# RWKV chain with both heads of a pair in one full-array TensorE product

## The chip, the cores and the metric

One core of a Trainium2 chip runs the whole program. The metric is device time in microseconds (us) of one execution; lower is better. A core has TensorE (matrix products, results in PSUM banks), VectorE, ScalarE and GpSimd, each with its own instruction queue, and SyncE, which issues the transfers.

## The reference, cut to what matters

One block of a streaming encoder on 512 tokens and 1024 channels: a norm, one input projection, an RWKV-7 branch (8 heads of 64) beside a gated DeltaNet branch (4 heads of 128), a gated merge, an output projection, a gated MLP with a short convolution, a final norm. All is float32. The change concerns the RWKV branch's recurrence:

```python
def step(S, inp):                        # S: (head, value 64, key 64), once per token
    r_t, w_t, k_t, v_t, a_t, b_t = inp
    sa = einsum('bhvk,bhk->bhv', S, a_t)
    S = S * w_t[:, :, None, :] + sa[..., None] * b_t[:, :, None, :] \
        + v_t[..., None] * k_t[:, :, None, :]
    y = einsum('bhvk,bhk->bhv', S, r_t)
    return S, y
...
y = group_norm_heads(y, ln_w, ln_b)      # mean and variance over the 64 channels of a head
y = y + jnp.sum(r_h * k_h * r_k, -1, keepdims=True) * v_h
```

## The kernel before, in words

Activations lie transposed: channels on partitions, 512 tokens along the free axis. The big products (`mm3`, lines 176, 177 and 179, called dense products below) split weights and activations into a high and a low fp32r part and add three products of 128x128 by 512 columns. `unit` fetches the weights and makes the parts `hi` (ScalarE, line 161) and `lo` (GpSimd or VectorE, line 163).

The recurrence is done in 8 chunks of 64 tokens. Two heads share the 128 partitions: head e ("even") on 0 to 63 (`lo`), head o on 64 to 127 (`hi`). A pair of heads is `hp`, 0 to 3; a group `g` is two pairs, and one chain runs over the chunks of both its pairs.
- `rwkv_prep` (steps R0 to R3) builds the operands of a pair: `ase` and `aso` (the decayed a and r of each head), `bkt` (b and k transposed), `ntb`, and the products of all token pairs in a chunk (lines 505 and 506: pair products, four chunks to a group, two groups to a pair of heads), masked by VectorE on line 512. Each of the two products uses 64 of the 128 rows.
- `rwkv_inverse` (steps i0, i1) inverts the triangular 64x64 matrix of every chunk and head and writes it back into `ntb`.
- `rwkv_chain` (steps c0, c1) runs over the chunks. Lines 626 and 627 centre the values (subtract the mean over the channels) and turn tokens to partitions. Per chunk there are three products that depend on one another: the first (639, 640) applies the operands to the state and the values, VectorE copies the result to `Z` (642); the second (645) applies the inverse, VectorE and ScalarE scale the result to U (647, 648); the third (651, 652) makes the next state, which VectorE scales and adds to a copy that ScalarE had scaled (636, 658). State and values lie in one tile for the even head and one for the odd. Lines 605 and 610 make the outputs, for four chunks at a time.

All four products of a step use a part of the array only: 64 columns of outputs (639, 640, 651, 652) or a 64x64 quarter (626, 627, 645):

```python
nc.tensor.matmul(pz[lo, 0, i, :], R[hp]["ase"][:, c, 0, :], se[:, i, 0, :], ...)   # 639
nc.tensor.matmul(pz[hi, 0, i, :], R[hp]["aso"][:, c, 0, :], so[:, i, 0, :], ...)   # 640
```

Before and after the RWKV chain, DeltaNet steps (G, I, C) and projections run. `ORDER` names the steps in program order, and the framework's scheduler writes each engine's queue from it: while the chain waits, TensorE's queue holds dense products of other steps. Waits between engines are put on whole tiles. A pair's operands lie in one buffer `R`, of which there are two (`RB`): the second group's steps and later the merge's gates (line 388) wait for them.

Of the kernel before, what the change touches and what calls it, by code (L numbers as in the profile page):

```python
# [9 lines left out]
F32 = mybir.dt.float32  # L10
# [83 lines left out]
class Body:  # L94
# [328 lines left out]
    def rwkv_prep(self, hp, first=None):  # L423
        nc = self.nc
        Rt, K, r = first or (self.rp.tile([128, 9, T], F32, tag="R", name=self.nm("R")), self.t("P"), self.t("P"))
        ase = Rt[:, 0:2, :].rearrange("p x t -> p (x t)").rearrange("p (c s t) -> p c s t", c=8, s=2)
        aso = Rt[:, 2:4, :].rearrange("p x t -> p (x t)").rearrange("p (c s t) -> p c s t", c=8, s=2)
        ntb = Rt[:, 4:6, :].rearrange("p x t -> p (x t)").rearrange("p (c s t) -> p c s t", c=8, s=2)
        bkt = Rt[:, 6:8, :].rearrange("p x t -> p (x t)").rearrange("p (c t) -> p c t", c=8)
        v = Rt[:, 8, :]  # L430
        if first is None:
            self.shifted(4 + hp, K)
            self.shifted(hp, r)
            self.shifted(8 + hp, v)
# [64 lines left out]
        for h in range(2):  # L499
            pe, po, pt = self.bank(), self.bank(), self.bank()  # L500
            for c in range(4):
                o = slice(c * 128, c * 128 + 128)
                cc = 4 * h + c
                bk = bkh[h][:, c, :, :].rearrange("p s t -> p (s t)")
                nc.tensor.matmul(pe[:, o], bk[0:64], ase[0:64, cc].rearrange("p s t -> p (s t)"), start=True, stop=True)
                nc.tensor.matmul(po[:, o], bk[64:128], aso[64:128, cc].rearrange("p s t -> p (s t)"), start=True, stop=True)
# [4 lines left out]
            for ps, s, tl in ((pe, lo, ntb), (pe, hi, ase), (po, hi, ntb), (po, lo, aso)):  # L511
                nc.vector.tensor_tensor(out=tl[s, w].rearrange("p c s t -> p c (s t)"),  # L512
                                        in0=ps[s, :].rearrange("p (c t) -> p c t", c=4),
                                        in1=rwm[s].unsqueeze(1).broadcast_to([64, 4, 128]), op=ALU.mult)
# [3 lines left out]
        return dict(ase=ase, aso=aso, ntb=ntb, bkt=bkt, v=v)  # L518
# [31 lines left out]
    def rwkv_inverse(self, g, R):  # L550
# [27 lines left out]
        for i, hp in enumerate(hps):  # L578
            ntb = R[hp]["ntb"]
            for q in range(4):  # L580
                s = slice(32 * q, 32 * q + 32)
                o = 32 * (q % 2)
                nc.scalar.activation(ntb[s, :, 0, o:o + 32].rearrange("p g (c j) -> p g c j", j=2), Y[s, 8 * i:8 * i + 8], AF.Copy)
            for b in (0, 64):
                nc.scalar.activation(ntb[b:b + 32, :, 0, 32:64], pfv[b:b + 32, 8 * i:8 * i + 8, :], AF.Copy)

    def rwkv_chain(self, g, R):
# [12 lines left out]
        def outputs(c0, kept):  # L600
            py = self.bank().rearrange("p (i c t) -> p i c t", c=4, i=2)
            for j, (e, o) in enumerate(kept):
                for i, hp in enumerate(hps):
                    for s, tl, a in ((lo, e, "ase"), (hi, o, "aso")):
                        nc.tensor.matmul(py[s, i, j, :], tl[:, i, 0, :], R[hp][a][:, c0 + j, 1, :],
                                         start=(j == 0 and i == 0), stop=False, skip_group_check=True)
            for j, (e, o) in enumerate(kept):
                for i, hp in enumerate(hps):
                    for s, tl in ((lo, e), (hi, o)):
                        nc.tensor.matmul(py[s, i, j, :], tl[s, i, 1, :], R[hp]["ntb"][s, c0 + j, 1, :],  # L610
# [5 lines left out]
        se, so = suv()  # L616
        nc.gpsimd.memset(se[lo, :, 0, :], 0.0)
        nc.gpsimd.memset(so[hi, :, 0, :], 0.0)
        kept = []
        for c in range(8):  # L620
            if c % 4 == 0:
                pv = self.bank().rearrange("p (c i t) -> p c i t", c=4, i=2)
                for c2 in range(4):
                    for i, hp in enumerate(hps):
                        vs = R[hp]["v"][:, (c + c2) * 64:(c + c2) * 64 + 64]
                        nc.tensor.matmul(pv[hi, c2, i, :], vs[lo], cent[lo, 0:64], start=True, stop=True)
                        nc.tensor.matmul(pv[lo, c2, i, :], vs[hi], cent[hi, 64:128], start=True, stop=True)
            c4 = c % 4
            kept.append((se, so))
            for tl, s in ((se, hi), (so, lo)):  # L630
# [438 lines left out]
```

## Time and profile before

| | |
|---|---|
| runs, median (lowest to highest) | 901.0 us (900.7 to 903.66) |
| the profiled execution | 901.19 us, span 899.4 us |
| TensorE busy | 866.2 us (96%) |
| VectorE, ScalarE, GpSimd busy | 590.1, 464.0, 195.4 us |
| mean granted TensorE clock | 0.992 of full |

The span is the time from the first to the last instruction. TensorE's ends are modelled, so the text reads its time from the starts of its products. A product on float32 operands appears as two records with a weight load each; one on fp32r as one. "128*64" in a row is the rows and columns of the array that a product uses.

### The profile page before, as it was taken

The numbers are of one execution on the slowest core, as the hardware profiler recorded it, in microseconds if no ns is written. First come the engines' busy times: TensorE is split into PE (matmuls) and PEld (weight loads), VectorE is DVE, ScalarE is ACT, GpSimd is POOL, SyncE is SP. The second block draws the span as 40 slices with busy tenths as digits, with TensorE's granted clock in tenths as the row PEclk, the third lists the DMA queues.
The fourth block names the chain that finished last, engine by engine and source line by source line (L and its number), as shares of the span: only waits on it lengthen the run. The fifth ranks groups of instructions, "written<-read, shape, count | busy, mean of one in ns | idle before, by whom it ended". The sixth has DMA issues, their size and how long they took to land.

```text
span 899.4 us, 13124 instructions
## 1 busy us (share of the span) xinstructions
PE 866.2 (96%) x4925; PEld 675.9 (75%) x4925; DVE 590.1 (66%) x1156; ACT 464.0 (52%) x879; POOL 195.4 (22%) x182
## 2 busy tenths in 40 slices
PE   7998999999999999999999999999999999999995
PEld 4776777666767777677787888888888888888885
DVE  6799797874888987855486448766666666312125
ACT  7654457667443776583534464444444444323233
POOL 2241123111121221111222213222222222222221
PEclk8999999999999999999999999999999999999998
DMA  6331222121212221135252223332223333223234
GB/s 238 119 105 60 71 71 72 48 72 48 71 59 71 71 72 36 60 113 181 94 188 94 94 76 111 95 94 94 94 94 94 99 103 96 88 88 105 89 106 136
DMA packets 28737, 84.76 MB, mean 94 GB/s; under 512 B 3200, under 2 KB 5376, under 8 KB 28672
## 3 DMA queue, kind: packets, MB, share of 16 engines
q1 hardware_dynamic: 28672, 83.91, 29.3%
q8 instruction: 39, 0.64, 0.3%
q14 instruction: 26, 0.21, 0.1%
HBM read 78.13 MB, written 5.77 MB: 93 GB/s over the span
## 4 chain that ended last, share of the span: by engine, by line
PE 73%; DVE 16%; ACT 4%; issue 3%; DMA 2%; POOL 1%; SPq 0%; DVEq 0%; POOLq 0%; ACTq 0%
PE D L179 20%; PE D L176 20%; PE D L177 20%; DVE R L512 1%; PE A L176 1%; PE A L177 1%; PE A L179 1%; DVE invN L541 1%; DVE lo L163 1%; DVE P L747 1%; DMA raw<-w_in 1%; DVE invY L543 1%; ACT hi L161 1%; DVE R L926 1%; PE B L639 1%
## 5 line engine op out<-in xcount | busy, mean ns | idle before, releaser
L163 POOL TENSOR_TENSOR lo<-raw,hi 128x512 fp32r<-128x512 f32 x133 | 179.8, 1352 | 649.7 <-ACT hi L161 625.8
L161 ACT ACTIVATE hi<-raw 128x512 fp32r<-128x512 f32 (+1 forms) x266 | 165.0, 622 | 257.3 <-PE D L179 193.5
L176 PE MATMUL D<-uh,lo 128*128 128x512 f32 (+1 forms) x456 | 184.0, 405 | 2.7 <-ACT uh L200 1.9
L177 PE MATMUL D<-uh,hi 128*128 128x512 f32 (+1 forms) x456 | 184.1, 405 | 0.0
L163 DVE TENSOR_TENSOR lo<-raw,hi 128x512 fp32r<-128x512 f32 (+1 forms) x133 | 92.4, 695 | 77.2 <-ACT hi L161 76.8
L176 PE MATMUL D<-u2h,lo 128*128 128x512 f32 x352 | 137.9, 392 | 0.0
L177 PE MATMUL D<-u2h,hi 128*128 128x512 f32 x352 | 137.8, 392 | 0.0
L179 PE MATMUL D<-ul,hi 128*128 128x512 f32 (+1 forms) x456 | 135.4, 403 | 0.4 <-DVE ul L198 0.4
L176 PEld LDWEIGHTS D<-uh,lo 128*128 128x128 f32 x456 | 86.2, 189 | 23.5 <-ACT uh L200 2.4
L177 PEld LDWEIGHTS D<-uh,hi 128*128 128x128 f32 x456 | 86.1, 189 | 18.8 <-issue 1.0
L179 PEld LDWEIGHTS D<-ul,hi 128*128 128x128 f32 x456 | 82.6, 188 | 19.6 <-issue 1.2
L179 PE MATMUL D<-u2l,hi 128*128 128x512 f32 x352 | 95.1, 392 | 0.0
L177 PEld LDWEIGHTS D<-u2h,hi 128*128 128x128 f32 x352 | 66.1, 188 | 14.9 <-issue 0.2
L176 PEld LDWEIGHTS D<-u2h,lo 128*128 128x128 f32 x352 | 66.1, 188 | 14.7 <-issue 0.2
L179 PEld LDWEIGHTS D<-u2l,hi 128*128 128x128 f32 x352 | 66.1, 188 | 14.1
L972 DVE SCALAR_TENSOR_TENSOR P<-T,vecs,P 128x511 f32<-128x511 f32 x88 | 69.0, 784 | 8.9 <-ACT P L970 2.8
L969 DVE TENSOR_TENSOR T<-D,acc 128x512 f32<-128x512 f32 x44 | 30.3, 690 | 49.8 <-PE D L179 45.8
L177 PE MATMUL D<-ah,hi 128*128 128x512 f32 (+1 forms) x126 | 45.2, 366 | 0.0
L176 PE MATMUL D<-ah,lo 128*128 128x512 f32 (+1 forms) x126 | 45.1, 366 | 0.0
L541 DVE TENSOR_TENSOR invN<-invA,invY 128x60 f32<-128x60 f32 (+24 forms) x124 | 33.2, 268 | 2.6
L543 DVE TENSOR_TENSOR invY<-invY,invN 128x60 f32<-128x60 f32 (+24 forms) x124 | 32.9, 266 | 2.9
L970 ACT ACTIVATE P<-T,vecs 128x512 f32<-128x512 f32 x44 | 31.8, 723 | 5.4 <-DVE T L969 1.9
(342 smaller groups left out, 1280.1 us busy)
## 6 DMA issues: line engine op xcount, KB each, us to landing
raw<-w_in SPq DMA_DIRECT2D x44, 512.0 KB, 3.6
raw<-ffn_up SPq DMA_DIRECT2D x44, 512.0 KB, 3.5
raw<-ffn_down SPq DMA_DIRECT2D x18, 512.0 KB, 3.5
raw<-w_out SPq DMA_DIRECT2D x8, 512.0 KB, 3.5
spill<-T SPq DMA_DIRECT2D x14, 256.0 KB, 2.0
R<-spill SPq DMA_DIRECT2D x14, 256.0 KB, 5.6
raw<-ffn_down SPq DMA_DIRECT2D x9, 384.0 KB, 3.0
xin<-xT SPq DMA_DIRECT2D x8, 256.0 KB, 5.7
```

Of the source, the lines that this page charges most:

```text
L161: nc.scalar.activation(hi[:, 0:w], raw[:, o:o + w], AF.Copy)
L163: self.on(str(self.halves % 4)).tensor_tensor(out=lo[:, 0:w], in0=raw[:, o:o + w], in1=hi[:, 0:w].bitcast(F32), op=ALU.subtract)
L176: nc.tensor.matmul(ps, wl[:, w[k]], x[k][0], start=(first and i == 0 and k == 0), stop=False)
L177: nc.tensor.matmul(ps, wh[:, w[k]], x[k][0], start=False, stop=False)
L179: nc.tensor.matmul(ps, wh[:, w[k]], x[k][1], start=False, stop=(last and i == len(parts) - 1 and k == n - 1))
L512: nc.vector.tensor_tensor(out=tl[s, w].rearrange("p c s t -> p c (s t)"), in0=ps[s, :].rearrange("p (c t) -> p c t", c=4), in1=rwm[s].unsq ...
L541: nc.vector.tensor_tensor(out=w, in0=rows[:, t, 0:t].unsqueeze(2).broadcast_to([128, t, n]), in1=Ym[:, t, c:G].unsqueeze(1).broadcast_to([ ...
L543: nc.vector.tensor_tensor(out=Ym[:, 0:t, c:G], in0=Ym[:, 0:t, c:G], in1=w, op=ALU.add)
L639: nc.tensor.matmul(pz[lo, 0, i, :], R[hp]["ase"][:, c, 0, :], se[:, i, 0, :], start=True, stop=True)
L969: nc.vector.tensor_tensor(out=h, in0=ps, in1=self.acc2, op=ALU.mult)
L970: nc.scalar.activation(cv, h, AF.Copy, scale=w(2))
L972: nc.vector.scalar_tensor_tensor(out=cv[:, sh:], in0=h[:, 0:T - sh], scalar=w(2 - sh), in1=cv[:, sh:], op0=ALU.mult, op1=ALU.add)
```

## The change

The even and the odd head now lie in one tile, so that one product over all 128 rows and 128 columns serves both heads of a pair; of its result only the two quarters on the diagonal are read. For the first product the operands of both heads lie side by side (`az`), and for the second the inverses are written into block-diagonal tiles `bd`, one per pair of a group, zeroed once. The pair products take all 128 rows, with the other head's rows zeroed first by GpSimd in each `R` buffer. Centring takes two chunks and both heads in one product. The copy to `Z` is split: VectorE the lower, ScalarE the upper half. The output products are as before.

```diff
@@ mixing
+        self.bd = [self.mp.tile([128, 8, 128], F32, name=f"bd{i}") for i in range(2)]
+        for bd in self.bd:
+            nc.gpsimd.memset(bd, 0.0)
@@ rwkv_prep
-        ase = Rt[:, 0:2, :].rearrange("p x t -> p (x t)").rearrange("p (c s t) -> p c s t", c=8, s=2)
-        aso = Rt[:, 2:4, :].rearrange("p x t -> p (x t)").rearrange("p (c s t) -> p c s t", c=8, s=2)
+        az = Rt[:, 0:4, :].rearrange("p x t -> p (x t)").rearrange("p (c s e t) -> p c s e t", c=8, s=2, e=2)
+        ase, aso = az[:, :, :, 0, :], az[:, :, :, 1, :]
...
+        nc.gpsimd.memset(ase[64:128], 0.0)
+        nc.gpsimd.memset(aso[0:64], 0.0)
...
-                nc.tensor.matmul(pe[:, o], bk[0:64], ase[0:64, cc].rearrange("p s t -> p (s t)"), start=True, stop=True)
-                nc.tensor.matmul(po[:, o], bk[64:128], aso[64:128, cc].rearrange("p s t -> p (s t)"), start=True, stop=True)
+                nc.tensor.matmul(pe[:, o], bk, ase[:, cc], start=True, stop=True)
+                nc.tensor.matmul(po[:, o], bk, aso[:, cc], start=True, stop=True)
@@ rwkv_inverse: the inverses go to self.bd[i] in place of ntb
-                nc.scalar.activation(ntb[b:b + 32, :, 0, 32:64], pfv[b:b + 32, 8 * i:8 * i + 8, :], AF.Copy)
+                nc.scalar.activation(bd[b:b + 32, :, b + 32:b + 64], pfv[b:b + 32, 8 * i:8 * i + 8, :], AF.Copy)
@@ rwkv_chain
         def suv():
-            return [self.mp.tile([128, 2, 2, 64], F32, tag=f"SUV{x}", name=self.nm("SUV"), bufs=6) for x in "eo"]
+            return self.mp.tile([128, 2, 2, 2, 64], F32, tag="SUV", name=self.nm("SUV"), bufs=6)
...
-                        nc.tensor.matmul(pv[hi, c2, i, :], vs[lo], cent[lo, 0:64], start=True, stop=True)
-                        nc.tensor.matmul(pv[lo, c2, i, :], vs[hi], cent[hi, 64:128], start=True, stop=True)
+                        vs = R[hp]["v"][:, (c + 2 * c2) * 64:(c + 2 * c2) * 64 + 128]
+                        nc.tensor.matmul(pv[:, c2, i], vs, cent, start=True, stop=True)
...
-                nc.tensor.matmul(pz[lo, 0, i, :], R[hp]["ase"][:, c, 0, :], se[:, i, 0, :], start=True, stop=True)
-                nc.tensor.matmul(pz[hi, 0, i, :], R[hp]["aso"][:, c, 0, :], so[:, i, 0, :], start=True, stop=True)
+                nc.tensor.matmul(pb[:, i], R[hp]["az"][:, c, 0].rearrange("p e t -> p (e t)"), x[:, :, i, 0, :], start=True, stop=True)
...
-            nc.vector.tensor_copy(z, pz[:, 0])
+            nc.vector.tensor_copy(z[lo], pb[lo, :, 0, :])
+            nc.scalar.activation(z[hi], pb[hi, :, 1, :], AF.Copy)
...
-                for s in (lo, hi):
-                    nc.tensor.matmul(pz[s, 1, i, :], R[hp]["ntb"][s, c, 0, :], z[s, i, :], start=True, stop=True)
+                nc.tensor.matmul(pu[:, i, :], self.bd[i][:, c, :], z[:, i, :], start=True, stop=True)
...
-                    nc.tensor.matmul(pz[lo, 2, i, :], R[hp]["bkt"][:, c, 0:64], se[:, i, 1, :], start=True, stop=True)
-                    nc.tensor.matmul(pz[hi, 2, i, :], R[hp]["bkt"][:, c, 64:128], so[:, i, 1, :], start=True, stop=True)
+                    nc.tensor.matmul(pb[:, i], R[hp]["bkt"][:, c, :], x[:, :, i, 1, :], start=True, stop=True)
```

In the changed file the first product is line 653, `Z` lines 655 and 656, the second product 658, U 660 and 661, the third product 664, centring 637, the pair products 511 and 512, the memsets 360, 435 and 436.

The scheduler places the chain's instructions anew. TensorE's queue, the second chunk of the first chain, from its first product (pz is in a bank B, the state in SUV, R are the buffers of the two pairs, D is a dense product's bank); before:

```order
L639 MATMUL B_1587<-SUV_1574,R_275 64x64
L640 MATMUL B_1587<-SUV_1575,R_275 64x64
L176 MATMUL D_1948<-uh,lo_1941 128x512
L639 MATMUL B_1587<-SUV_1574,R_567 64x64
L177 MATMUL D_1948<-uh,hi_1940 128x512
L640 MATMUL B_1587<-SUV_1575,R_567 64x64
L176 MATMUL D_1948<-uh,lo_1941 128x512
L177 MATMUL D_1948<-uh,hi_1940 128x512
L176 MATMUL D_1948<-uh,lo_1941 128x512
L645 MATMUL B_1587<-Z_1592,R_275 64x64 x2
L645 MATMUL B_1587<-Z_1592,R_567 64x64 x2
```

and now:

```order
L653 MATMUL B_1576<-SUV_1564,R_275 128x128
L179 MATMUL D_1886<-ul,hi_1878 128x512
L653 MATMUL B_1576<-SUV_1564,R_573 128x128
L179 MATMUL D_1886<-ul,hi_1878 128x512 x2
L176 MATMUL D_1886<-uh,lo_1883 128x512
L177 MATMUL D_1886<-uh,hi_1882 128x512
L176 MATMUL D_1886<-uh,lo_1883 128x512
L177 MATMUL D_1886<-uh,hi_1882 128x512
L658 MATMUL B_1576<-Z_1579,bd_473 128x64
L658 MATMUL B_1576<-Z_1579,bd_474 128x64
```

The first product stood in three pieces and stands in two; between its last piece and the second product there were three dense products and are six.

ScalarE's queue in the fourth chunk of the same chain, now (T and hi are casts and copies of other steps, WS the scaled copy of the state):

```order
L646 ACTIVATE WS_1623<-SUV_1616,wc 64x64 [waits DVE_49] x4
L656 ACTIVATE Z_1631<-B_1628 64x128 [waits DVE_49,Activation_49]
L641 ACTIVATE SUV_1642<-B_1647 64x256 [waits PE_49]
L412 ACTIVATE T_1950<-D_1925 128x512 [waits PE_49]
L161 ACTIVATE hi_2002<-raw_1996 128x512
```

Z's upper half is new here; it waits for VectorE and stands behind the four scaled copies. Before, Z was on VectorE alone.

GpSimd's queue near the end of the second preparation (lo are low halves of weights), now:

```order
L163 TENSOR_TENSOR lo_581<-raw_578,hi_580 128x512
L435 MEMSET R_573 64x16x64
L436 MEMSET R_573 64x16x64
L163 TENSOR_TENSOR lo_618<-raw_615,hi_617 128x512
L360 MEMSET bd_473 128x1024
L163 TENSOR_TENSOR lo_655<-raw_652,hi_654 128x512
L360 MEMSET bd_474 128x1024
```

Before, the three low halves followed one another with three short memsets between the last two.

## Rows read from the trace of the kernel before

**Rows 1.** The page's first lines: the span, and each engine's busy time, its share of the span and its instructions.

```profile
span 899.4 us, 13124 instructions
PE 866.2 (96%) x4925; PEld 675.9 (75%) x4925; DVE 590.1 (66%) x1156; ACT 464.0 (52%) x879; POOL 195.4 (22%) x182
```

**Rows 2.** Busy us of PE, PEld, DVE, ACT and POOL (instructions in brackets) in four stretches, then the granted TensorE clock, the DMA share and GB/s.

```profile
40.00:60.00 20.00, 19.06 (x85) 14.65 (x84) 18.90 (x28) 11.85 (x20) 8.87 (x11) 1.00 0.34 104
...
160.00:215.00 55.00, 54.37 (x479) 37.38 (x480) 36.84 (x134) 35.71 (x98) 7.76 (x11) 1.00 0.19 59
215.00:330.00 115.00, 108.56 (x704) 81.89 (x702) 99.97 (x215) 65.37 (x122) 20.22 (x18) 1.00 0.21 67
330.00:390.00 60.00, 58.10 (x586) 41.02 (x585) 44.98 (x151) 40.02 (x107) 8.36 (x13) 1.00 0.17 51
```

**Rows 3.** TensorE's groups by line and shape: count, busy us, mean ns of one record.

```profile
L640 PE MATMUL B<-SUV,R 128*64 128x64 f32 x64 | 9.9, 244 | 0.0
...
L645 PE MATMUL B<-Z,R 64*64 64x64 f32 x128 | 8.0, 231 | 0.3
```

**Rows 4.** TensorE's timeline round a third product: start us, length us, then line, operation and count.

```profile
173.90 0.39 PE L177 MATMUL D<-uh,hi 128*128 128x512 f32 x1
174.23 0.27 PE L651 MATMUL B<-SUV,R 128*64 128x64 f32 x1
...
174.61 0.50 PE L176 MATMUL D<-uh,lo 128*128 128x512 f32 x1
174.95 0.39 PE L177 MATMUL D<-uh,hi 128*128 128x512 f32 x1
```

**Rows 5.** The same round the first product of the second chunk, the last two of its three pieces.

```profile
169.29 0.49 PE L176 MATMUL D<-uh,lo 128*128 128x512 f32 x1
169.71 0.33 PE L639 MATMUL B<-SUV,R 128*64 128x64 f32 x2
169.97 0.51 PE L177 MATMUL D<-uh,hi 128*128 128x512 f32 x1
170.41 0.33 PE L640 MATMUL B<-SUV,R 128*64 128x64 f32 x2
170.67 0.51 PE L176 MATMUL D<-uh,lo 128*128 128x512 f32 x1
171.01 0.39 PE L177 MATMUL D<-uh,hi 128*128 128x512 f32 x1
```

**Rows 6.** The same round two full-array products of the DeltaNet chain.

```profile
265.30 0.40 PE L177 MATMUL D<-uh,hi 128*128 128x512 f32 x1
265.53 0.39 PE L885 MATMUL B<-vn,G 128*128 128x128 f32 x2
265.76 0.39 PE L888 MATMUL B<-G,vn 128*128 128x128 f32 x2
265.90 0.48 PE L176 MATMUL D<-uh,lo 128*128 128x512 f32 x1
266.22 0.39 PE L177 MATMUL D<-uh,hi 128*128 128x512 f32 x1
```

**Rows 7.** The same round a centring, 32 records of lines 626 and 627.

```profile
157.77 0.27 PE L626 MATMUL B<-cons,R 64*64 64x64 f32 x1
...
158.85 0.50 PE L176 MATMUL D<-uh,lo 128*128 128x512 f32 x1
```

**Rows 8.** The same round a group of pair products (16 records of lines 505 and 506) and its transposes (line 508).

```profile
98.08 0.40 PE L179 MATMUL D<-ul,hi 128*128 128x512 f32 x1
98.40 0.37 PE L505 MATMUL A<-R,BK 64*128 64x128 f32 x1
...
98.62 0.27 PE L505 MATMUL A<-R,BK 64*128 64x128 f32 x1
98.73 0.27 PE L505 MATMUL A<-R,BK 64*128 64x128 f32 x1
...
99.73 0.66 PE L508 MATMUL A<-cons,BK 128*128 128x128 f32 x4
100.14 0.94 PE L179 MATMUL D<-ul,hi 128*128 128x512 f32 x3
100.92 0.40 PE L176 MATMUL D<-uh,lo 128*128 128x512 f32 x1
```

**Rows 9.** The longest wait of TensorE's weight loads in the whole span: who waited for whom, us in total, times, longest.

```profile
PEld B L651 <- ACT SUV L648: 5.7, 11, 1.0
```

**Rows 10.** Groups of the other engines by line: count, busy us, mean ns of one, idle us ahead and what ended it.

```profile
L642 DVE COPY Z<-B 128x128 f32<-128x128 f32 x16 | 4.6, 290 | 9.4 <-PE B L640 9.2
L636 ACT ACTIVATE WS<-SUV,wc 64x64 f32<-64x64 f32 x48 | 16.6, 345 | 4.7 <-DVE SUV L661 2.2 <-DVE SUV L658 1.6
L631 ACT ACTIVATE SUV<-B 64x256 f32<-64x256 f32 x32 | 12.0, 376 | 3.4 <-PE B L627 3.0
L648 ACT ACTIVATE SUV<-B,rs 64x64 f32<-64x64 f32 x32 | 9.9, 308 | 16.7 <-DVE SUV L647 16.1
L290 POOL MEMSET lora_l<- 64x512 f32 x2 | 1.0, 518 | 0.3 <-POOLq L1060 0.3
```

**Rows 11.** The last reload of the merge's gates on SyncE's timeline, and the first use of a gate by VectorE (times of one in ns, first and last start in us).

```profile
418.08 0.32 SPq L388 DMA_DIRECT2D R<-spill  x1
L924 DVE SCALAR_TENSOR_TENSOR R<-R,A x8: 683/688/689, 437.0 to 454.4; 128x512 f32<-128x512 f32 x8
```

More of the change, by code (lines that the diff above doesn't have):

```diff
@@ L577, in rwkv_inverse @@
                                      Y[b + 32:b + 64, 8 * i + c], start=True, stop=True)
-        for i, hp in enumerate(hps):
-            ntb = R[hp]["ntb"]
+        for i in range(2):
+            bd = self.bd[i]
             for q in range(4):
                 s = slice(32 * q, 32 * q + 32)
-                o = 32 * (q % 2)
-                nc.scalar.activation(ntb[s, :, 0, o:o + 32].rearrange("p g (c j) -> p g c j", j=2), Y[s, 8 * i:8 * i + 8], AF.Copy)
+                nc.scalar.activation(bd[s, :, 32 * q:32 * q + 32].rearrange("p g (c j) -> p g c j", j=2), Y[s, 8 * i:8 * i + 8], AF.Copy)
             for b in (0, 64):
-                nc.scalar.activation(ntb[b:b + 32, :, 0, 32:64], pfv[b:b + 32, 8 * i:8 * i + 8, :], AF.Copy)
+                nc.scalar.activation(bd[b:b + 32, :, b + 32:b + 64], pfv[b:b + 32, 8 * i:8 * i + 8, :], AF.Copy)
     def rwkv_chain(self, g, R):
@@ L614, in outputs @@
                                      py[:, i], AF.Copy)
-        se, so = suv()
-        nc.gpsimd.memset(se[lo, :, 0, :], 0.0)
-        nc.gpsimd.memset(so[hi, :, 0, :], 0.0)
+        eo = ((0, lo, hi), (1, hi, lo))
+        x = suv()
+        for e, s, _ in eo:
+            nc.gpsimd.memset(x[s, e, :, 0, :], 0.0)
         kept = []
@@ L621, in rwkv_chain @@
             if c % 4 == 0:
[L622 to L623 removed]
+                pv = self.bank().rearrange("p (c i e t) -> p c i e t", c=2, i=2, e=2)
+                for c2 in range(2):
                     for i, hp in enumerate(hps):
[L625 to L631 removed]
+                        vs = R[hp]["v"][:, (c + 2 * c2) * 64:(c + 2 * c2) * 64 + 128]
+                        nc.tensor.matmul(pv[:, c2, i], vs, cent, start=True, stop=True)
+            kept.append(x)
+            tok = (lo, hi)[c % 2]
+            for e, _, s in eo:
+                nc.scalar.activation(x[s, e], pv[tok, c % 4 // 2, :, e, :].unsqueeze(2).broadcast_to([64, 2, 2, 64]), AF.Copy)
             if c and c < 7:
@@ L634, in rwkv_chain @@
                 for i, hp in enumerate(hps):
-                    for tl, s in ((se, lo), (so, hi)):
-                        nc.scalar.activation(ws[s, i, :], tl[s, i, 0, :], AF.Copy, scale=self.wc[s, hp, c:c + 1])
-            pz = self.bank().rearrange("p (x i t) -> p x i t", x=4, i=2)
+                    for e, s, _ in eo:
+                        nc.scalar.activation(ws[s, i, :], x[s, e, i, 0, :], AF.Copy, scale=self.wc[s, hp, c:c + 1])
+            pz = self.bank()
+            pb = pz[:, 0:256].rearrange("p (i e t) -> p i e t", i=2, e=2)
@@ L653, in rwkv_chain @@
-                ne, no = suv()
+                    nc.tensor.matmul(pb[:, i], R[hp]["bkt"][:, c, :], x[:, :, i, 1, :], start=True, stop=True)
+                nx = suv()
                 for i, hp in enumerate(hps):
-                    for tl, s in ((ne, lo), (no, hi)):
+                    for e, s, _ in eo:
                         w = self.wc[s, hp, c:c + 1]
                         if c:
-                            nc.vector.scalar_tensor_tensor(out=tl[s, i, 0, :], in0=pz[s, 2, i, :], scalar=w, in1=ws[s, i, :],
+                            nc.vector.scalar_tensor_tensor(out=nx[s, e, i, 0, :], in0=pb[s, i, e, :], scalar=w, in1=ws[s, i, :],
@@ L665, in rwkv_chain @@
             if c < 7:
-                se, so = ne, no
+                x = nx
     def rwkv_out(self, hps, R):
```

28 lines of the change are left out of this document (14 added, 14 removed).

## The prediction

> **What bounds the kernel now.** I read the page's engine shares first, then the stretches, then the TensorE groups, then single stretches of its timeline. TensorE is busy 866.2 us of a span of 899.4 us [rows 1]. In the three stretches in which the RWKV chains run (160 to 215 and 330 to 390 us) and between them, it is busy 54.37 of 55, 58.10 of 60 and 108.56 of 115 us, while VectorE and ScalarE stay at 36.84 to 99.97 and 35.71 to 65.37 us there [rows 2]. So a microsecond that leaves TensorE's queue there leaves the span, as long as the dense products that stand between the chain's steps cover the chain's own waits. The reader is to see in the timeline that a busy TensorE is not equally useful everywhere: around each group of small tiled products it loses time that no instruction of the group accounts for.
>
> A dense product is issued every 0.23 us (265.30 to 265.53 us [rows 6]). I price a group of small products as the time from the start of the last dense product ahead of it to the start of the second one behind it, less 0.47 us for two dense products. Every float32 product is issued as two halves: the 32 first products of line 640 are 64 records, the 64 products of line 645 are 128 [rows 3].
> - Four tiled products (8 halves): 173.90 to 174.95 us, 1.05 us, so **0.58 us** [rows 4]. The halves themselves take 0.38 us (174.23 to 174.61); the other 0.20 us lies at the two edges.
> - One tiled product alone (2 halves): 169.97 to 171.01 us, 1.04 us, so **0.57 us** as well; with only one dense product between it and the next piece, 169.29 to 169.97 us less 0.23, 0.45 us [rows 5]. A tiled product costs the same alone as in fours.
> - Two full-array products (4 halves; the DeltaNet chain's lines 885 and 888): 265.30 to 266.22 us, 0.92 us, so **0.45 us** [rows 6]. There the halves take 0.37 us, 0.09 each with the last one cut short by the next group; I take 0.11 for a half inside a longer run, which gives 0.23 us for one full-array product.
>
> **The change part by part.** *Chain steps.* Each chunk has three products for both head pairs; four tiled products become two full-array ones. The second of them now multiplies a 128-column stationary tile with 64 columns instead of 128; I leave it at the same 0.45 us, since no row here shows less. I counted the groups that stand alone between dense products in the two orders.
> - First product: before 23 pieces at 0.45 to 0.57 us, 0.5 taken, 11.5 us; now 18 pieces at 0.23, 4.1 us. Minus 7.4.
> - Third product: before 11 groups at 0.58, 6.4 us; now 13 at 0.45, 5.9 us. Minus 0.5.
> - Second product: before 9 groups at 0.58 and 3 pieces at 0.5, 6.7 us; now 12 at 0.45, 5.4 us. Minus 1.3.
> - Centring: 16 tiled products take 1.08 us (157.77 to 158.85) and 0.20 at the edges [rows 7]; 4 full-array ones take 8 x 0.11 and 0.05. Minus 0.35, four times: 1.4.
> - The steps that stand inside larger groups (beside the output products, which stay tiled): those lose pieces too but gain edges between full and tiled neighbours. Bounds 0 and minus 4; I take minus 2, the middle.
>
> Together **minus 12.6 us**.
>
> *Pair products.* Lines 505 and 506 run on two halves of the rows, side by side: a pair of halves every 0.11 us (98.62 to 98.73 [rows 8]). As full-array products each half takes 0.11 alone: 8 x 0.11, 0.9 us more for each of the 8 groups, 7.1 us, and that is the upper end. Against it the edges: the group with its transposes costs 98.08 to 100.92 us less four dense products, 1.91 us; 16 halves at 0.11, the transposes' 0.41 and 0.1 at the edges give 2.3, 0.4 more, 3.2 us in all, the lower end. I take 0.5 a group, nearer to the lower end because rows 8 are the very group: **plus 4.0 us**.
>
> *GpSimd.* Ten new memsets of 1,024 columns. A 64x512 one takes 0.52 us [rows 10], so about 1 us each (an estimate by twice the columns), 10 us on an engine that is busy 195.4 of 899.4 us [rows 1]. Four of them stand in GpSimd's queue ahead of the low halves of weights that TensorE needs near 40 to 60 us, where GpSimd is busy 8.87 of 20 us and VectorE 18.90 [rows 2]; the last four stand ahead of another low half, waiting for the first group's buffers. Cost 0 to 4, **plus 1 us** taken. Without the slack of that queue it would be all four, 4 us.
>
> *The copy of Z.* One 128x128 copy on VectorE, 0.29 us, becomes a 64x128 one there and one on ScalarE [rows 10], which the order lets wait for VectorE's. So the step from first to second product grows by one ScalarE instruction, 0.31 us by the 64x64 scalings there (line 648), 16 times. What is queued behind it on ScalarE are casts of weights and the scaled copies of U; TensorE waits for it before the second product. I cost it at nothing because 4 to 9 dense products (0.9 to 2.1 us) now stand between the two steps in the order where 3 or 4 stood; if that cover is gone it is 16 x 0.35, 5.6 us. The 16 copies are 5 us more on ScalarE, which has 19 us free in the first chain's stretch [rows 2].
>
> *Waits of the chain.* Its largest wait today, before the third product, is 5.7 us [rows 9]; its four serial scalings are unchanged. Taken as unchanged, minus 3 to plus 5.
>
> *Later end.* The chains end 19 to 20 dense products later in the order. Then the merge's buffers come free later, about 4 us. Their last reload is issued at 418.08 us and first used at 437.0 us [rows 11], so this is hidden; without it, 4 us.
>
> **Sum:** minus 12.6, plus 4.0, plus 1.0: minus 7.6 us. The profiled execution took 901.19 us, so 893.6; the median of the runs is 901.0, the same within 0.2. I say **893.5 us**.
>
> The Trainium skill (TensorEngine Tiling (Array Packing), section Theoretical Speedup) speaks against this change: a dimension of at most 64 should be packed as tiles, up to two times faster for each such dimension. The same page's Key Properties say that a change of tiling mode drains TensorE. The trace agrees with both: 0.11 us for a pair of halves [rows 8], and 0.20 us at the edges of four [rows 4]. By the packing rule alone the sum would be plus 15 us (third rival), by the rows it is minus 7.6.
>
> **Rivals.**
> - *Waits take the place.* The chain becomes its own bound and TensorE stands before the second product, 16 x 0.35 us: 893.5 + 5.6, 899. For it: VectorE in front of Z serves the inverse of the other branch in the same stretches. Against it: the 3 to 4 dense products covered that step today, and the new order leaves more. Chance 0.15.
> - *Slower, by ScalarE's queue.* Z's upper half stands behind up to four scaled copies (0.345 us each) and a copy of U (0.376) [rows 10], all released with the first product. If these run ahead of it every time, Z comes 1.76 + 0.3 = 2.1 us after its input; today it is a group's 0.38 us [rows 4] and the copy's 0.29, 0.7 us. That is 1.4 us later, and if no dense product covers it, 16 x 1.4 is 22 us: 916. It decides from 0.5 us of wait a chunk (8 us over 16, which eats the gain). Against it: the scaled copies are released one by one as their inputs come, and 0.9 to 2.1 us of dense work stands there. Chance 0.07.
> - *Packing was worth more.* If the edges cost nothing, or come back at the full-array groups, only array time counts. The chain's 496 halves at 0.034 (32 in 1.08 us [rows 7]), 17 us, become 216 at 0.11, 24 us; with the pairs' 7.1 and GpSimd's 1 that is 15 us more: 916. This is what the packing rule of the Trainium skill (TensorEngine Tiling (Array Packing), Theoretical Speedup) would make of it. Rows 4 to 6 speak against it: full-array groups of the same type have edges of 0.08 us, not 0.20. Chance 0.04.
> - *More than the sum.* The waits inside the chain's groups go as well, and the steps beside the output products save their full 4 us: 887 and below, to 883. Chance 0.06.
>
> **How the numbers follow.** My forecast, 893.5 with a range of its own from 887 (larger groups minus 4, pairs 3.2, no cost of memsets, waits minus 3) to 898 (pairs 7.1, memsets plus 2), has 0.68. The range of 886 to 901 takes in the forecast and the first rival, 0.83 in all, and leaves out the slower two and part of the last. A measurement here can tell about 0.3% from no change, that is 898.3 to 903.7 us. Faster: 0.68 and 0.06, 0.74. Same: 0.15. Slower: 0.07 and 0.04, 0.11.
>
> **What would show it.** In the new profile, TensorE's records for the four chain steps should number 216 instead of 496; two products of a chain step between dense ones should cost about 0.45 us and a single one about 0.25; the pair products should come one half every 0.11 us and their group with transposes cost about 2.3 us. From the first chain's first step to its last the dense products should be issued closer. VectorE and ScalarE should change by less than 6 us. It would be wrong if TensorE stood idle before the second product, if the full-array groups showed 0.2 us at their edges, or if GpSimd's memsets made the dense products near 50 us wait for a low half.

## The result and the profile after

The change made the kernel slower: 911.2 us median (910.55 to 912.05, 4 runs) beside 901.0 for the kernel before, a ratio of 1.011 [1.0092, 1.0128], 10 us. Forecast were 893.5 us (886 to 901). The profiled execution of the changed kernel has a span of 909.7 us.

The page's first lines, in the form of [rows 1]:

```profile
span 909.7 us, 12613 instructions
...
PE 867.5 (95%) x4645; PEld 687.9 (76%) x4645; DVE 589.9 (65%) x1156; ACT 465.9 (51%) x893; POOL 203.4 (22%) x192
```

TensorE has 280 records fewer, as forecast (496 to 216 in the chain), and is 1.3 us busier. VectorE and ScalarE moved by less than 2 us, GpSimd by 8.0. The four stretches of [rows 2] (busy us and instructions of PE, PEld, DVE, ACT, POOL; clock, DMA share, GB/s):

```profile
40.00:60.00 20.00, 17.91 (x68) 13.30 (x67) 19.93 (x26) 11.34 (x20) 10.24 (x14) 0.91 0.37 120
160.00:215.00 55.00, 50.67 (x315) 38.59 (x315) 40.98 (x141) 38.36 (x103) 8.93 (x16) 1.00 0.19 58
215.00:330.00 115.00, 109.26 (x687) 84.29 (x686) 92.81 (x211) 62.08 (x118) 21.83 (x23) 0.99 0.20 62
330.00:390.00 60.00, 55.08 (x451) 42.10 (x450) 46.85 (x149) 43.65 (x116) 10.44 (x15) 1.00 0.17 54
```

TensorE was idle 0.6 and 1.9 us in the chains' two stretches before; now it is idle 4.3 and 4.9 us. These are the same times and not the same work, for the change is some 4 us late at 110 us already. From 40 to 60 us it lost another microsecond, and the granted clock fell to 0.91. Its chain groups by line and shape, as in [rows 3] (count, busy us, mean ns | idle us ahead and what ended it):

```profile
L653 PE MATMUL B<-SUV,R 128*128 128x128 f32 x64 | 14.5, 314 | 1.3 <-DVE SUV L670 1.0 <-ACT SUV L641 0.3
L658 PE MATMUL B<-Z,bd 128*128 128x64 f32 x64 | 10.5, 287 | 3.9 <-ACT Z L656 3.8
L664 PE MATMUL B<-SUV,R 128*128 128x128 f32 x56 | 9.5, 293 | 1.5 <-ACT SUV L661 1.3
L637 PE MATMUL B<-cons,R 128*128 128x128 f32 x32 | 4.9, 281 | 0.0
```

And the waits of its weight loads, whose longest was [rows 9] before (total us, times, longest). The last two rows are the largest for the second product in the kernel before; all six of its rows there make 5.0 us:

```profile
PEld B L658 <- ACT Z L656: 9.1, 15, 1.3
PEld B L664 <- ACT SUV L661: 4.8, 9, 1.1
```

```profile
PEld B L645 <- issue: 1.6, 5, 0.4
PEld B L645 <- DVE invY L543: 1.5, 4, 0.4
```

The second product (L658) waits for Z's upper half, the copy that is new on ScalarE, in 15 of 16 chunks. Part of that runs beside products issued earlier: TensorE itself is idle 3.9 us ahead of L658, as its row says. How that comes about, in the chunk from 181.97 us. TensorE (start us, length us, line, operation, count, idle ahead):

```profile
182.51 0.49 PE L653 MATMUL B<-SUV,R 128*128 128x128 f32 x2
182.76 0.48 PE L176 MATMUL D<-uh,lo 128*128 128x512 f32 x1
183.08 0.39 PE L177 MATMUL D<-uh,hi 128*128 128x512 f32 x1
183.31 0.39 PE L176 MATMUL D<-uh,lo 128*128 128x512 f32 x1
183.54 0.40 PE L177 MATMUL D<-uh,hi 128*128 128x512 f32 x1
183.77 0.63 PE L179 MATMUL D<-ul,hi 128*128 128x512 f32 x2
184.76 0.66 PE L658 MATMUL B<-Z,bd 128*128 128x64 f32 x4 [0.35 <-ACT Z L656]
```

VectorE and ScalarE in the same stretch:

```profile
182.91 0.68 DVE L163 TENSOR_TENSOR lo<-raw,hi 128x512 fp32r<-128x512 f32 x1
183.63 0.28 DVE L655 COPY Z<-B 64x128 f32<-64x128 f32 x1
...
182.61 1.41 ACT L646 ACTIVATE WS<-SUV,wc 64x64 f32<-64x64 f32 x4
184.03 0.38 ACT L641 ACTIVATE SUV<-B 64x256 f32<-64x256 f32 x1
184.43 0.27 ACT L656 ACTIVATE Z<-B 64x128 f32<-64x128 f32 x1
```

The first product is issued by 182.73. A low half of weights (0.68) stands in front of Z on VectorE; four scaled copies (1.41) and a copy of the next centred values (0.38) stand in front of it on ScalarE. Z is whole 2.0 us after its product, and six dense products cover only 1.4 of them.

The pair products, as in [rows 8]:

```profile
102.17 0.40 PE L179 MATMUL D<-ul,hi 128*128 128x512 f32 x1
102.41 0.40 PE L511 MATMUL A<-R,BK 128*128 128x128 f32 x2
102.65 0.39 PE L512 MATMUL A<-R,BK 128*128 128x128 f32 x2
...
104.21 0.60 PE L514 MATMUL A<-cons,BK 128*128 128x128 f32 x4
104.57 0.95 PE L179 MATMUL D<-ul,hi 128*128 128x512 f32 x3
105.35 0.40 PE L176 MATMUL D<-uh,lo 128*128 128x512 f32 x1
```

From 102.17 to 105.35 less four dense products: 2.25 us a group, 1.91 before, 2.3 forecast.

I priced all of TensorE's groups by the prediction's rule (from the last dense product ahead to the second behind, less 0.47 us), and put what is left between two dense products into waits and half clock. Half clock is a stretch with the granted clock at its lower level (0.5 of full, 1.2 GHz). The sums are differences to the kernel before, in us (chain before: 59.5; up to 0.8 us is left over where a group lies in a half-clock stretch):

```
kernel                          chain  pairs  other  half clock  waits   span
the change                       -0.7   +2.7   -0.2     +1.3      +7.2  +10.3
e2: chain part alone             -0.7   +0.6   +0.7     +2.2      +2.2   +5.0
e5: e2, Z on VectorE             -4.7   +1.3   +2.6     +2.5      -0.1   +1.4
e6: e5, U scaled by VectorE      -4.5   +3.1   +1.9     -1.1      +0.6   -0.7
e12: centring alone               +0.2    0     +2.4     +1.1      -0.9   +2.6
```

The chain's groups, 59.5 us, were to lose 12.6; they lost 0.7. The column of the pairs also moves in e2, e5 and e6, whose pair products are those of before; that much of it is waits and half clock inside these groups. The waits of the change between dense products are four, priced from start to start: 2.15 us at 311.4, 1.89 at 52.3, 1.60 at 37.3 and 1.13 at 234.7.

The longest of them stands between the two chains, where no step of a chain is near. TensorE, VectorE, and the windows round it (columns as in [rows 2]):

```profile
313.83 0.47 PE L176 MATMUL D<-uh,lo 128*128 128x512 f32 x1 [1.99 <-DVE P L759]
```

```profile
309.98 0.74 DVE L759 SCALAR_TENSOR_TENSOR P<-D,vecs,P 128x511 f32<-128x511 f32 x1
...
312.94 0.74 DVE L759 SCALAR_TENSOR_TENSOR P<-D,vecs,P 128x509 f32<-128x509 f32 x1
```

```profile
304.00:314.00 10.00, 8.01 (x34) 6.03 (x33) 9.58 (x21) 9.21 (x14) 2.02 (x2) 1.00 0.08 27
314.00:319.00 5.00, 5.00 (x16) 3.91 (x16) 4.01 (x9) 1.02 (x3) 0.00 (x0) 0.66 0.49 156
```

A DeltaNet step (L759) frees the bank of the next dense product late, and 3.4 us at the lower clock follow. From the 810th to the 850th dense product the change loses 3.6 us by it, and e2, e13 and e15 below lose 3.7 each. The other kernels lose nothing there, among them all that copy Z on VectorE alone. So it comes with the order that the scheduler makes when Z's upper half is on ScalarE (e10 has that too, and another order); which shift does it isn't shown.

### The profile page after: what moved, and what is told of

Its sections match the earlier page's. It is cut to its first block, busy times and chain, and to the rows that moved or that the text cites. A ratio compares the mean times of both kernels' runs of the same rounds, so it can differ in the third digit from the quotient of the medians.

```text
span 909.7 us, 12613 instructions
## 1 busy us (share of the span) xinstructions
PE 867.5 (95%) x4645; PEld 687.9 (76%) x4645; DVE 589.9 (65%) x1156; ACT 465.9 (51%) x893; POOL 203.4 (22%) x192
## 4 chain that ended last, share of the span: by engine, by line
PE 60%; DVE 9%; ACT 6%; issue 2%; POOL 1%; DMA 0%; DVEq 0%; ACTq 0%; POOLq 0%; SPq 0%
PE D L179 17%; PE D L177 17%; PE D L176 17%; ACT hi L161 1%; DVE invN L547 1%; DVE R L938 1%; DVE invY L549 1%; PE A L177 1%; PE A L176 1%; DVE lo L163 1%; PE A L179 1%; PE B L658 1%; PE B L653 1%; DVE BK L492 0%; ACT uh L200 0%
## 5 line engine op out<-in xcount | busy, mean ns | idle before, releaser
L547 DVE TENSOR_TENSOR invN<-invA,invY 128x60 f32<-128x60 f32 (+24 forms) x124 | 35.1, 283 | 2.6
```

The source lines that it names most:

```text
L547: nc.vector.tensor_tensor(out=w, in0=rows[:, t, 0:t].unsqueeze(2).broadcast_to([128, t, n]), in1=Ym[:, t, c:G].unsqueeze(1).broadcast_to([ ...
```

## The experiments

All ratios are to the kernel before on the same chip, whose medians lay between 900.7 and 901.7 us.

**Taking the change apart: e1, e2, e4, e8.** e1 is the kernel before with the pair products as full-array ones and their eight memsets; e4 has all ten memsets and nothing else; e8 only the two of the block-diagonal tiles. e2 is the change less the pair products:

```diff
 e2 (from the change)
-        nc.gpsimd.memset(ase[64:128], 0.0)
-        nc.gpsimd.memset(aso[0:64], 0.0)
-                nc.tensor.matmul(pe[:, o], bk, ase[:, cc], start=True, stop=True)
+                nc.tensor.matmul(pe[:, o], bk[0:64], ase[0:64, cc], start=True, stop=True)
...
 e8 (from the kernel before; e4 also has the two lines above in rwkv_prep)
+        self.bd = [self.mp.tile([128, 8, 128], F32, name=f"bd{i}") for i in range(2)]
+        for bd in self.bd:
+            nc.gpsimd.memset(bd, 0.0)
```

e1: 

> The kernel before with one part of the change: the pair products as full-array products over all rows, with the memsets of the other head's rows; chain and centring as before. The pair groups cost 2.7 us more in the changed kernel's trace than in that of before. Theory A (the chain's waits on ScalarE's half of Z and on the alternating scalings ate the gain): these groups and the memsets cost about 3 us, so 904 us. Theory B (pair products and memsets are what made the change slower): about 909 us or more.

e2: 

> The changed kernel with the pair products packed on half the rows again and without the memsets in the R buffers; chain, centring and block-diagonal inverses stay. Theory A: still slower than before, 911.2 less 2.7 for the pairs and 1 to 2 for the memsets, about 907 us, with some 9 us of TensorE waits for Z. Theory B: at 900 us or below, since the chain's groups themselves cost less.

e4: 

> The kernel before with the ten new memsets alone: the other head's rows of each R buffer, and the two block-diagonal tiles, which nothing reads here. Theory A: hidden on GpSimd but for the stretch near 50 us, 901 to 903 us. Theory B: the memsets delay low halves of weights and share the memory port with VectorE, 905 us or more.

e8: 

> The kernel before with the two memsets of the block-diagonal tiles alone (the tiles are not used). With these and the eight memsets of the R tiles it took 906.4 us. If the cost lies in the two large memsets, in GpSimd's queue ahead of low halves of weights near 50 us: 905 us or more. If it lies in the eight: 902 us or less.

Measured: e1 908.3 us, 1.0075 [1.0046, 1.0105]; e2 906.2, 1.0039 [1.0026, 1.0052]; e4 906.4, 1.0048 [1.003, 1.0066]; e8 901.2, 0.999 [0.9977, 1.0003]. Here and below, costs are taken from the ratios. So the memsets cost 4.3 us, none of it by the two large ones (e8): theory B's time in e4; the way it comes about follows below. The pair products themselves cost e1 less e4, 2.4 us, known to some 3 us either way; e1 at 908.3 lies nearer theory B than A. The chain part costs 3.5 us where a gain of 12.6 was forecast (e2: theory A). The parts add up, within these intervals: 6.8 (e1) and 3.5 (e2) are 10.3, and the whole is 10. In the traces the groups with pair products take 25.7 us in e1 and 22.0 in the kernel before, 3.7 more.

The Trainium skill (TensorEngine Tiling (Array Packing), Theoretical Speedup) would keep two products of 64 rows packed, at up to twice the speed. For the pairs the traces agree in sign: a half every 0.11 us where a pair of halves took 0.11 [rows 8], and 2.25 us a group where it took 1.91. The times by themselves don't show it.

**The chain part: e3, e5, e6, e7.** e3 (from the change) and e5 (from e2) copy all of Z on VectorE. e6 is e5 with two scalings of U in place of four; e7 puts the same edit into the kernel before.

```diff
 e3, e5
-            nc.scalar.activation(z[hi], pb[hi, :, 1, :], AF.Copy)
+            nc.vector.tensor_copy(z[hi], pb[hi, :, 1, :])
 e6 (e7 alike)
-            for i, hp in enumerate(hps):
-                nc.vector.tensor_scalar_mul(x[lo, 0, i, 1, :], pu[lo, i, :], self.rs2[lo, hp, c:c + 1])
-                nc.scalar.activation(x[hi, 1, i, 1, :], pu[hi, i, :], AF.Copy, scale=self.rs2[hi, hp, c:c + 1])
+            rs = self.rs2[:, 2 * g:2 * g + 2, c].unsqueeze(2).broadcast_to([128, 2, 64])
+            for e, s in enumerate((lo, hi)):
+                nc.vector.tensor_tensor(out=x[s, e, :, 1, :], in0=pu[s], in1=rs[s], op=ALU.mult)
```

e3: 

> The changed kernel with both halves of Z copied by VectorE, so that the second product waits for one engine. Theory A: the wait for Z (9.1 us of TensorE's weight loads in the changed kernel) falls to 3 us or less, so 903 to 906 us. Theory B: no change, 910 to 912 us. If VectorE's own queue is what delays Z, also near 911 us.

e5: 

> The chain part of the change alone (block-diagonal tiles and their memsets, full-array chain products and centring), pair products packed as before, no memset of the R tiles, and the copy of Z in two halves on VectorE alone. With Z's upper half on ScalarE the same kernel took 906.2 us (before 901.4). Theory A, the step through ScalarE to Z is what the chain part loses: with it gone TensorE's chain groups fall by the 4 us seen with the whole change, 902 us or less. Theory B, the wait at Z was only one place for it: what is saved there comes back elsewhere, 905 us or more.

e6: 

> The kernel with the chain part alone and Z on VectorE, and the scaling of U written as two 64x128 products with a broadcast scale on VectorE instead of four 64x64 ones that VectorE and ScalarE take in turn (1.3 us a chunk in the trace of the change, from 179.09 to 180.41). Theory C, a chunk lasts as long as its own loop through VectorE and ScalarE: some 0.6 us less in each of 16 chunks, about 8 to 10 us below the kernel with Z on VectorE alone, so 892 to 897 us. Theory D, the loop lies behind dense products and TensorE's own time decides: within 2 us of that kernel, 900 us or more.

e7: 

> The kernel before, with only the scaling of U changed: two 64x128 products with a broadcast scale on VectorE instead of four 64x64 ones in turn on VectorE and ScalarE. Theory C, the chain's loop through VectorE and ScalarE sets the length of a chunk in the kernel before too: 16 x 0.5 us less, 892 to 895 us. Theory D, the tiled products on TensorE set it there: 900 to 902 us.

Measured: e3 911.0 us, 1.0124 [1.008, 1.0168]; e5 902.4, 1.0004 [0.999, 1.0017]; e6 900.0, 0.9977 [0.9961, 0.9994]; e7 909.6, 1.0072 [1.0051, 1.0094]. In the chain part alone Z on VectorE gives back 3.2 us (e5 against e2), as theory A has it. The wait before the second product, in e5:

```profile
PEld B L655 <- DVE Z L653: 3.4, 10, 0.6
```

It was 9.1 us in e2, and the chain's groups cost 4.0 us less. But that is mostly not where the time came back. From the 410th to the 810th dense product, the first chain and what follows it, e2 and e5 take the same within 0.2 us: what the chain's groups save, other groups cost more. From the 850th to the 1,300th, with the second chain, e5 gains 1.6 us and loses as much at 483 us to a half-clock stretch. The place between the chains, absent in e5, is 3.7 us. So Z's step through ScalarE is shown to slow the chain's groups, and the order that comes with it to cost the time; the two are not separated. In the whole change (e3: 911.0, theory B's time) Z on VectorE gave nothing that can be measured: its trace, the fastest of its four runs, has the 4.0 us as well and a wait at Z of 3.3, and a wait of 2.97 us at 233.0 where the change had one of 1.13.

e6 and e7 test whether a chunk's own loop sets the time (theory C). The loop did get shorter. Seven chunks of the first and the second chain, the dense products among them, and the rest when these are taken at 0.231 us:

```
              first chain            second chain
before     46.1 us, 110, 20.7     47.8 us,  92, 26.5
change     51.4 us, 130, 21.4     48.6 us, 106, 24.1
e5         47.1 us, 122, 18.9     47.4 us, 103, 23.6
e6         38.7 us,  86, 18.8     41.2 us,  76, 23.6
e7         35.6 us,  72, 18.9     43.9 us,  67, 28.4
```

In e6 a chunk lasts 1.0 us less than in e5, and the rest, TensorE's own time in the chain, is the same. The dense products that filled the chunk are done elsewhere, so the time fell by 2.4 us and not by 8 to 10. Even of that the traces lay 1.5 us to a half-clock stretch at 483 us that e5's has and e6's has not (see the end); by the 1,300th dense product e6 is 0.4 us ahead. Theory C falls; nor does D hold as put, for e7 got slower. e7 is 3.2 us ahead of the kernel before at the 900th dense product and 6.4 behind at the 1100th. In between lies this, on ScalarE, on TensorE, and in the three windows (columns as in [rows 2]) round it:

```profile
396.73 0.63 ACT L161 ACTIVATE hi<-raw 128x512 fp32r<-128x512 f32 x1
397.39 0.78 ACT L839 ACTIVATE invA<-B 32x256 f32<-32x256 f32 x2
```

```profile
397.81 0.31 PE L842 MATMUL B<-invN,invA 32*32 32x32 f32 x2 [2.15 <-ACT invA L839]
```

```profile
383.00:397.00 14.00, 12.47 (x80) 9.19 (x79) 9.67 (x25) 10.78 (x23) 2.63 (x2) 1.00 0.51 166
397.00:411.00 14.00, 13.19 (x97) 10.02 (x98) 4.72 (x6) 6.02 (x15) 1.27 (x1) 0.52 0.47 167
411.00:425.00 14.00, 14.00 (x84) 10.97 (x84) 5.72 (x16) 2.86 (x5) 1.28 (x1) 0.99 0.35 108
```

With the dense products moved, TensorE stood 2.15 us for a small copy behind a cast, and the granted clock was at its lower level for 14 us behind that. The loop saved time, and the new order lost more; that the clock fell because of that wait is not shown.

**The memsets: e9, e10, e13, e15.** The view that found their cost is the start time (us) of the dense product that has n others ahead of it, called the n-th here:

```
   n   before  change  e8 bd   e9 first two  e15 first two   e6
                       only    only          on VectorE
 100    37.4    35.8    35.8      35.9          35.2         37.3
 170    55.8    58.6    54.2      58.7          53.6         55.7
 300   103.7   108.2   103.5     106.6         105.4        106.1
1100   430.9   440.7   430.7     433.8         438.1        429.9
1800   595.4   605.6   595.6     598.4         603.0        594.8
```

From the 100th to the 170th the kernel before takes 18.4 us and every kernel with the first tile's memsets on GpSimd, and no further edit at the start, 21 to 23. ScalarE's timeline of the change shows why:

```profile
26.15 1.15 ACT L161 ACTIVATE hi<-raw 128x512 fp32r<-128x512 f32 x2 [6.53 <-DMA raw<-w_in]
27.32 1.28 ACT L191 ACT_TABLE_LOAD   x1
28.61 0.69 ACT L191 ACTIVATE P<-A,cons 128x512 f32<-128x512 f32 x1
```

Two casts of a weight block stand ahead of the input norm's 1/rms (L191, L192) and wait 6.53 us for their transfer. The 1/rms starts at 28.61 us, at 25.47 in the kernel before and at 23.32 in e15 below. The normalised input comes later by that, VectorE has almost no idle time left from 48 us on, and TensorE waits at 52.3 us for the halves of the input. In the change, e3, e4 and e9 a half-clock stretch of 3.4 us follows that wait, about 1.5 us of the loss; in e1 none does. The four kernels:

```diff
 e9 (from the kernel before; in rwkv_prep)
+        if hp == 0:
+            nc.gpsimd.memset(ase[64:128], 0.0)
+            nc.gpsimd.memset(aso[0:64], 0.0)
 e10 (from the change; e15 the same for hp == 0 alone)
-        nc.gpsimd.memset(ase[64:128], 0.0)
-        nc.gpsimd.memset(aso[0:64], 0.0)
+        nc.vector.memset(ase[64:128], 0.0)
+        nc.vector.memset(aso[0:64], 0.0)
 e13 (from the change)
-        self.rstd(acc, r)
+        with self.tc.high_priority():
+            self.rstd(acc, r)
```

e9: 

> The kernel before with two memsets of 64x1024 on GpSimd alone, those of the first head pair's tile, at the very start; what they zero is overwritten later or not read. Theory E, the cost of the memsets is no time of GpSimd but the order: with these two the scheduler puts two casts of weights (line 161) ahead of the norm's 1/rms (lines 191 and 192) in ScalarE's queue; the casts wait for their transfer until about 26 us, and all that needs the norm comes 3 to 4 us later. Then these two alone cost what all ten cost, 905 to 907 us, with the 1/rms at 28.5 us or later. Theory F, the later memsets do it, among low halves of weights near 50 us and in front of the second pairs' tiles: 900 to 902 us.

e10: 

> The whole change, with the eight memsets of the R tiles on VectorE instead of GpSimd; nothing else differs in the source. The order of ScalarE's queue at the start is then that of the kernel before, the 1/rms ahead of the two casts. Theory E: 4 to 5 us less than the change's 911, 906 to 907 us, though VectorE gets 8 us of memsets. Theory F: 910 us or more.

e13: 

> The whole change, its memsets untouched; only the norm's 1/rms (lines 191 and 192) gets priority, so that ScalarE does it ahead of the two casts of weights that wait for their transfer. Theory E, the place of the 1/rms is what the memsets cost: the 170th dense product starts near 55 us instead of 58.6, and the time falls by about 3.5 to 4 us from 911, to 907 to 908. Theory F, the memsets cost GpSimd's own time further on: 910 us or more.

e15: 

> The whole change with only the first head pair's two memsets moved, from GpSimd to the start of VectorE's queue; the other six stay on GpSimd, and the product of the norm stays where it was on TensorE. Theory E: the 1/rms is ahead of the casts again, the 170th dense product starts at 54 to 56 us instead of 58.6, and the time is 3 to 4 us below 911, 907 to 908. Theory F, the later memsets cost as well or instead: 909 us or more, or the gain at 58 us gone by 75 us.

Measured: e9 904.4 us, 1.0041 [1.0025, 1.0057], the 1/rms at 28.73 us; e10 915.7, 1.0156 [1.0128, 1.0184]; e13 913.1, 1.014 [1.0119, 1.0161]; e15 908.2, 1.0078 [1.0048, 1.0108]. Two memsets in an idle stretch of GpSimd cost 3.7 us in e9, nearly all that the ten cost. In e15 ScalarE has the old order again:

```profile
23.32 0.69 ACT L191 ACTIVATE P<-A,cons 128x512 f32<-128x512 f32 x1 [3.13 <-PE A L217]
...
25.32 0.63 ACT L192 ACTIVATE P<-P 128x512 f32<-128x512 f32 x1
25.86 0.62 ACT L161 ACTIVATE hi<-raw 128x512 fp32r<-128x512 f32 x1
```

The whole change is 3.0 us faster by it: theory E. The two intervals overlap, so the start times carry this more than the times do. They also show a part of theory F's sign: of 5.0 us ahead of the change at the 170th product 2.7 are left at the 230th, near 78 us, for e15 has a half-clock stretch from 69.3 to 72.8 us, behind a wait of 1.85 us that the change has too, without one. The two that missed show the same thing from the other side. e13 pulled the norm's product forward on TensorE too, where it waited for VectorE:

```profile
21.70 1.12 PE L217 MATMUL A<-P,cons 128*128 128x512 f32 x2 [2.25 <-DVE P L212]
```

e10 won 3.6 us on the change by the 170th product and lost most of them at 67 us. There the bank that the next dense product needs is freed by L351, behind seven operations of the pair preparation on VectorE:

```profile
70.77 0.47 PE L176 MATMUL D<-uh,lo 128*128 128x512 f32 x1 [2.79 <-DVE R L351]
```

```profile
65.26 2.90 DVE L492 SCALAR_TENSOR_TENSOR BK<-P,sp,T 64x256 f32<-64x256 f32 x4
68.27 0.69 DVE L494 TENSOR_TENSOR P<-P,T 128x512 f32<-128x512 f32 x1
68.99 0.85 DVE L497 TENSOR_TENSOR BK<-P,T 64x256 f32<-64x256 f32 x2
69.88 0.75 DVE L351 SCALAR_TENSOR_TENSOR R<-D,vecs,R 128x511 f32<-128x511 f32 x1
```

TensorE stands for L351 once more, 3.25 us at 254 us, with a half-clock stretch behind it. What makes e10 some 4 us slower than the change in all isn't settled.

**Mending the whole: e11, e14, e16; one part alone: e12.** e11 is e10, e14 is e13 and e16 is e15, each with the edits of e5 and e6 (Z and U on VectorE). e12 is the kernel before with the centring alone as full-array products:

```diff
 e12 (from the kernel before)
-                        nc.tensor.matmul(pv[hi, c2, i, :], vs[lo], cent[lo, 0:64], start=True, stop=True)
-                        nc.tensor.matmul(pv[lo, c2, i, :], vs[hi], cent[hi, 64:128], start=True, stop=True)
+                        nc.tensor.matmul(pv[:, c2, i], vs, cent, start=True, stop=True)
...
```

e11: 

> The whole change with the three places mended that the runs so far point to: memsets of the R tiles on VectorE, Z copied by VectorE alone, U scaled by two 64x128 products on VectorE. If the losses add up as single parts: the 900.0 of the chain part with Z and U mended, plus 1.5 to 2 for the pair products, 901 to 903 us. If the order of the whole decides more than the parts: 905 us or more, or below 899.

e14: 

> The whole change with the 1/rms ahead of the casts, Z copied by VectorE alone and U scaled by two 64x128 products on VectorE; the memsets stay on GpSimd. If the parts add up: 900.0 for the chain part so mended, 1.5 to 2 for the pair products, 901 to 903 us. If a new wait comes with the whole: 905 us or more.

e16: 

> The whole change with the first pair's memsets on VectorE, Z copied by VectorE alone and U scaled by two 64x128 products on VectorE. If the parts add up: the 900.0 of the chain part so mended, 1.5 to 2 for the pair products, 901 to 903 us. If a new wait comes with the whole: 905 us or more.

e12: 

> The kernel before with one part of the change alone, the centring of values as 4 full-array products for 16 tiled ones, four times. By the prediction's term 1.4 us less, 900 us. If a shift of the order eats it: 901 us or more.

Measured: e11 908.0 us, 1.0069 [1.0047, 1.0092]; e14 907.3, 1.0084 [1.0057, 1.011]; e16 903.7, 1.0025 [1.0008, 1.0043]; e12 904.6, 1.0035 [1.0022, 1.0048]. With the start in order (e16) the mends of Z and U take 4.8 us more off the change, and what stays above e6 is 4.3 us for the pair products and their later memsets, where 1.5 to 2 were expected; about 1.5 of it is a half-clock stretch at 484.6 us that e16's trace has and e6's has not. With the new waits of e10 and e13 the whole stays at 907 to 908. The centring saved what it should where it stands alone (one group 1.28 to 0.90 us), but the chain's sum did not fall (+0.2 in the table above) and the groups of other work cost 2.4 us more; which shift of the order did that isn't settled, and a half-clock stretch at 483.8 us adds some 1.5. The one version that beats both kernels is e6: the chain part alone, pair products packed, Z and U on VectorE, by 2.1 us [0.5, 3.5].

## Why the prediction was wrong

- **First product**, minus 7.4: 18 pieces cost 6.9 us and not 4.1, against 11.0 before: minus 4.1. Most pieces take 0.29 to 0.42 us; 0.23 was the price inside a run, and a lone product was put at it without edges.
- **Second product**, minus 1.3: 10.7 us and not 5.4, against 7.2 before: plus 3.5. The shortest two groups take 0.52 us, so the product's price was near; the rest is the wait for Z. With Z on VectorE (e5) it is 8.2.
- **Third product**, minus 0.5: 9.6 us and not 5.9, against 7.7: plus 1.9. Four groups take 0.44 to 0.45, the price as put; the others wait for U.
- **Centring and larger groups**, minus 3.4: minus 2.0.
- **The failed step** is the cover: "I cost it at nothing because 4 to 9 dense products now stand between the two steps", and the waits "taken as unchanged". The prices of the second and third product held where nothing waits, that of the lone first product did not. But the order holds a fixed number of dense products there, and the step grew to 2.0 us. TensorE stood idle before the second product, which the prediction names as a sign of being wrong. Of the 11.9 us that the chain's groups are short of minus 12.6, the second product is 4.8, the third 2.4, the first 3.3 and the rest 1.4. The second rival named this very queue, its 2.1 us, and 0.5 us a chunk as the point from which it decides; the second product's weight loads wait 9.1 us over 16 chunks, 0.57. It got a chance of 0.07, though its durations stood in [rows 10] and its order among the rows quoted. That 911.2 came out near its 916 is luck all the same: the memsets and the pair products are 6.7 us of it, and the step was partly covered.
- **Outside the chain's groups** the sum has no term for the 3.6 us between the chains, a wait in another step and half clock behind it. The chain part is plus 3.5 by e2 though its groups lost 0.7, and this place is most of the difference.
- **GpSimd**, plus 1 (0 to 4): plus 4.3, and by another way. The prediction priced memsets by their queue. What they cost is a new order of ScalarE's queue at the start, which the order of the two programs showed and the prediction passes over, since no edit stood there.
- **Pair products**, plus 4.0 (3.2 to 7.1): the group came out at 2.25 us as forecast (2.3), all eight 3.7 us longer in e1's trace, within the bounds. The time, plus 2.4 (e1 less e4), is known to some 3 us and can't tell.
- The **later end** was hidden, as put: the 1,100th dense product is 9.8 us late and the 1,800th 10.2, so little is lost behind the chains.

By the runs the parts are plus 3.5, plus 4.3 and plus 2.4: plus 10.2 us where minus 7.6 was put, the first two known to 1 to 2 us, the third to 3.

## What to carry to other kernels

A shorter product on a busy engine is a gain only where the step behind it keeps up: price the hop to the next product, with all that stands in front of it in each queue, before the product. A product's price inside a run is not its price alone: 0.23 us became 0.29 to 0.42. Where a scheduler sets the order, read the whole order of both programs, the start first, for it moves instructions far from the edit; two memsets on an idle engine cost 3.7 us here. The start time of the n-th dense product, side by side for two kernels, shows at once in which stretch the time went, and here it put 3.6 us where no edited step stands.

## What was not expected of the hardware

The same wait of TensorE, 1.93 to 1.95 us idle, ending between 481.8 and 495.7 us, stands in all kernels, but only in some (e3, e5, e7, e11, e12, e16) is the clock at its lower level (1.2 GHz) for 3.4 us behind it. e12, before and behind that wait:

```profile
478.00:483.50 5.50, 3.61 (x16) 2.58 (x14) 4.14 (x5) 1.79 (x4) 1.09 (x1) 1.00 0.19 54
483.50:488.50 5.00, 4.95 (x15) 3.93 (x16) 2.79 (x4) 2.40 (x4) 1.27 (x1) 0.66 0.28 102
```

From the 1,300th to the 1,500th dense product these kernels take 50.3 to 50.4 us and the others 48.8: 1.5 us for one such stretch, about half of what some of these edits moved. What decides whether the clock falls there, the traces don't show.
